# A Strassen MLP trunk: sums of weights and of squares moved to GpSimd, gating done straight from PSUM, the last products paired, and TensorE's order written out

## The chip, the core and the metric

The kernel runs on one core of one Trainium2 chip. The metric is device time in microseconds for one execution, the median of several runs. TensorE is PE in the rows (its weight loads PEld), VectorE is DVE, ScalarE is ACT, GpSimd is POOL, SyncE, which issues the DMAs, is SP.

## What is computed

One layer of a hybrid decoder trunk for 1024 prompt tokens and 32 sample tokens (8 sequences of 4), model width 1024, all in float32:

```python
h = rmsnorm(x, norm_mix_g) * (1 + sc1) + sh1
proj = h @ w_in                       # conv, gated recurrence and window attention heads
...                                   # the three head groups -> out_a, out_b, out_c
mix = jnp.concatenate([out_a, out_b, out_c.astype(x.dtype)], axis=-1) @ w_out
x = x + g1 * mix
h2 = rmsnorm(x, norm_mlp_g) * (1 + sc2) + sh2
x = x + g2 * (jnp.square(jax.nn.relu(h2 @ w_up)) @ w_down)
...
y_prompt = rmsnorm(xp, final_g)
```

The gates g1, g2 and the shifts are one vector for the whole prompt and one for each sample sequence. The change concerns what begins with `@ w_out`; the projection and the head groups ahead of it are not edited.

## The kernel before

Activations lie transposed in SBUF: a tile of [128, 8, 1056] holds 8 rows of 128 channels by 1056 tokens (1024 prompt, then 32 sample). The matrix products from `w_out` on are cut into nine **phases** of 1024 x 1024 weights: one for `w_out` ("out"), and four pairs for the MLP, up0, down0, up1, down1, up2, down2, up3, down3. Each phase is one level of Strassen's scheme: seven products of half size instead of eight, done in the order `SEQ = (2, 1, 6, 7, 4, 5, 3)`, each for four groups j of 128 output channels, so 28 **units** (p, j) in a phase. A float32 product is made of three reduced-precision matmuls (high x high, high x low, low x high, lines 1266 to 1268), for 4 blocks i of the inner dimension and 2 halves of 264 tokens: 24 matmuls in a unit, 672 in a phase.

Around each unit stands `prep`, which prepares what later units need:

- `w_unit(u)` splits the weights of unit u into a high and a low part (an ACT cast, line 1232, and a DVE subtraction, line 1233), three units ahead. Four such buffers rotate, so the weights of unit u+3 are split when product u-1 is done.
- `t_unit(p, i)` makes the activations of a product and splits them (ACT line 1252, DVE line 1253). Product 6 needs two further DVE subtractions, and a third that updates a block for product 4 (line 1255). The four up phases share their activations: up0 stores the split parts to HBM and up1 to up3 load them.
- `w_sums(ch)` makes Strassen's combinations of the weight blocks A, B, C, D in place, E = A - C, C = C + D, A = C - A, B = B - A (lines 1223 to 1226), for two halves ch of the columns, 1024 elements in each of 128 partitions. Products 6, 7 (E), 5 and 3 use the results.

`update` takes a product out of PSUM: an ACT copy for the first into a block in the phases that open a buffer, a DVE addition (line 1351) otherwise. PSUM is four buffers of two banks (pool `pp`).

In the out phase the result is added up in `hb`, and `gated` (line 1356) then adds g1 * hb to x, which is kept in `xr`. `norm2_square` squares it on ACT and adds up the squares on DVE (lines 1370 to 1374); `norm2(th)` turns the sums of one half th of the tokens into the reciprocal root (six small matmuls at line 1380, a DVE copy, two GpSimd instructions at lines 135 and 136, a DVE product `dg` with the identity, and a matmul with ones that spreads it over the partitions), and applies it to the eight rows (DVE line 1401, ACT line 1402) to give the input of up0 in `big_m`. `norm2(0)` is called after the first unit of product 5 of out, `norm2(1)` after the first unit of up0.

In down3 the products are gated into x, and the last rows are transposed back (line 1463), squared, normalised and stored, tile by tile of 128 tokens (`final_part`). The last product runs in two halves of 264 tokens.

The order of instructions on every engine comes from a scheduler that simulates engines and queues when the program is built. It may place an instruction ahead of others that come earlier in the code where it finds it ready. On the chip each engine works its list off in order.

Just ahead of the out phase stands the last part of the input projection, the gate of the recurrence (`evac_g`, lines 496 to 499), whose PSUM and scratch memory the phases then take over (`p1.close()`).

Of the kernel before, what the change touches and what calls it, by code (L numbers as in the profile page):

```python
# [19 lines left out]
P = 128  # L20
# [23 lines left out]
def kernel(  # L44
# [440 lines left out]

    def evac_g(h):
        def f_(c, ps):
# [701 lines left out]
    BLOCK = {"A": (0, 0), "B": (1, 0), "C": (0, 1), "D": (1, 1)}  # L1189

# [8 lines left out]

    class Phase:  # L1200
        def __init__(self, w, row0, col0, src=None, stored=None, keep=False, first=False):
            self.w, self.row0, self.col0 = w, row0, col0
            self.src, self.stored, self.keep, self.first = src, stored, keep, first
            self.raw, self.wu, self.tt = {}, {}, {}

        def w_tile(self, role):
            if role == ("B" if self.first else "E"):
                return rp.tile([P, D], F32, tag="wr", name="wr")
            return env["w2"].tile([P, D], F32, tag="wq", name="wq")

        def w_load(self, role):
            kh, nh = BLOCK[role]
            for ch in range(2):
                t = v3(self.w_tile(role), 256)
# [5 lines left out]
        def w_sums(self, ch):  # L1220
            a, b, c, d = (self.raw[r, ch] for r in "ABCD")
            e = self.raw["E", ch] = v3(self.w_tile("E"), 256)
            tt(out=e, in0=a, in1=c, op=ALU.subtract)
            tt(out=c, in0=c, in1=d, op=ALU.add)
            tt(out=a, in0=c, in1=a, op=ALU.subtract)  # L1225
            tt(out=b, in0=b, in1=a, op=ALU.subtract)

        def w_unit(self, u):
            p, j = SEQ[u // 4], u % 4
# [4 lines left out]
            self.wu[u] = t  # L1234
            if u in (5, 7):
                self.w_sums(u // 2 - 2)

        def t_unit(self, p, i):
# [15 lines left out]
            if p == 6:  # L1254
                tt(out=b21, in0=b21, in1=s, op=ALU.subtract)
# [16 lines left out]
    def bank2():  # L1272
        return env["pp"].tile([P, 1024], F32, tag="pp", name="pp")
# [4 lines left out]
    def flow(ph, nxt, update, order=None, after=lambda p, j: None, early=lambda u: None):  # L1278

        ps = {}  # L1280
        for i, p in enumerate(SEQ):
            for j in range(4):
                u = 4 * i + j
                if order is None or i < 5:
                    fresh = p in (2, 1, 5)
                    if fresh:
                        ps[j] = bank2()
                    ph.product(ps[j], p, j, fresh)
                    prep(ph, nxt, u)
                    update(p, j, ps[j])  # L1290
                    after(p, j)
        if order is not None:
            order(ph, nxt)

    def prep(ph, nxt, u):
        i, j = u // 4, u % 4
        q, v = (ph, i + 1) if i < 6 else (nxt, 0)
        if q is not None:
            q.t_unit(SEQ[v], j)
        q, v = (ph, u + 3) if u + 3 < 28 else (nxt, u + 3 - 28)  # L1300
        if q is not None:
            q.w_unit(v)
        if nxt is not None:
            for at, role in ((13, "B"), (18, "A"), (22, "C"), (25, "D")):
# [4 lines left out]
    ph_o = Phase(w_out, 0, 0, src=big_m, first=True)  # L1309
    for i, (w, fn) in enumerate(plan):  # L1310
# [15 lines left out]
    for u in range(3):  # L1326
        ph_o.w_unit(u)
# [258 lines left out]
```

## Time and profile before

| | us |
|---|---|
| median of 3 runs | 1295.61 (1294.93 to 1298.15) |
| the profiled execution, own time | 1299.38 |
| its span, first to last instruction | 1297.5 |
| matmul busy time | 1238.5 (95% of the span) |
| DVE, ACT, POOL busy | 907.6, 557.0, 69.1 |

The profiled execution lies 3.77 us above the median. Times within it are counted from its first instruction. The nine phases begin at 482.84 us. Matmuls overlap in the records, so that the spacing of their starts, not their recorded length, says how fast TensorE goes.

### The profile page before, as it was taken

To read this page: it belongs to the slowest core of one execution; us is meant where nothing else is said; L and a number is where in the kernel's file an instruction comes from. 1 tells how busy PE (TensorE), PEld (TensorE's weight loads), DVE (VectorE), ACT (ScalarE), POOL (GpSimd) and SP (SyncE) were. 2 spreads that over 40 slices of the span, in tenths; PEclk is the share of its full clock that TensorE was granted. 3 is DMA by queue.
4 is the path that set the end of the run, shared out by engine and by line. 5 is a ranking of instruction groups with operands and counts; after the bars stand their busy time and mean duration, and the time that the engine had idled before them with its cause. 6 is when DMAs were issued, how large, how long until landed. Compare 5 with 4: busy or idle time off the path is not lost.

```text
span 1297.5 us, 26603 instructions
## 1 busy us (share of the span) xinstructions
PE 1238.5 (95%) x10994; PEld 1170.4 (90%) x10994; DVE 907.6 (70%) x1651; ACT 557.0 (43%) x1127; POOL 69.1 (5%) x139
## 2 busy tenths in 40 slices
PE   8999999999999978985999999999999999999896
PEld 6889988888887978985999999999999999999896
DVE  4779995675746667697859554497643986528986
ACT  5622212433532343654665524553245632446332
POOL 3400000101200000000000000000000000000002
PEclk9999999999999999997999999999999999999899
DMA  8934333233132135222750275501666138561003
GB/s 272 366 106 125 99 102 96 76 107 96 56 99 85 36 137 176 86 99 115 298 200 18 66 248 205 196 17 50 203 230 216 34 99 282 207 227 50 1 1 135
DMA packets 116780, 172.44 MB, mean 133 GB/s; under 512 B 10877, under 2 KB 90835, under 8 KB 116636
## 3 DMA queue, kind: packets, MB, share of 16 engines
q1 hardware_dynamic: 116660, 170.74, 39.4%
q8 instruction: 87, 1.43, 0.5%
q14 instruction: 33, 0.27, 0.1%
HBM read 139.82 MB, written 32.13 MB: 133 GB/s over the span
## 4 chain that ended last, share of the span: by engine, by line
PE 73%; DVE 16%; DMA 5%; issue 3%; ACT 2%; SPq 1%; POOL 1%; DVEq 0%; ACTq 0%; POOLq 0%
PE pp L1268 13%; PE pp L1266 13%; PE pp L1267 13%; PE psg L157 7%; PE psg L158 7%; PE psg L159 7%; DVE tu L1253 3%; DMA wq<-in_w_down_dram 3%; DVE wu L1233 3%; PE pa_bank L259 2%; DVE xr L1351 1%; PE pso L849 1%; PE pso L622 1%; DVE wq L1225 1%; DVE t L1249 1%
## 5 line engine op out<-in xcount | busy, mean ns | idle before, releaser
L1266 PE MATMUL pp<-tu,wu 128*128 128x264 f32 x2016 | 580.6, 289 | 21.9 <-DVE H L497 7.3
L1267 PE MATMUL pp<-tu,wu 128*128 128x264 f32 x2016 | 580.6, 288 | 6.6 <-DVE tu L1253 6.6
L1268 PE MATMUL pp<-tu,wu 128*128 128x264 f32 x2016 | 578.2, 288 | 2.2 <-DVE wu L1233 2.1
L1266 PEld LDWEIGHTS pp<-tu,wu 128*128 128x128 f32 x2016 | 385.3, 191 | 24.9 <-issue 15.6
L1267 PEld LDWEIGHTS pp<-tu,wu 128*128 128x128 f32 x2016 | 385.5, 191 | 8.0 <-DVE tu L1253 7.9
L1268 PEld LDWEIGHTS pp<-tu,wu 128*128 128x128 f32 x2016 | 385.6, 192 | 4.1 <-DVE wu L1233 3.9
L1233 DVE TENSOR_TENSOR wu<-wq,wu 128x512 fp32r<-128x512 f32 x212 | 145.4, 687 | 107.6 <-ACT wu L1232 107.1
L1232 ACT CAST wu<-wq 128x512 fp32r<-128x512 f32 x212 | 130.8, 619 | 134.1 <-PE pp L1268 117.8
L157 PE MATMUL psg<-hh,wh 128*128 128x352 f32 x544 | 180.3, 333 | 0.7 <-ACT wh L148 0.7
L158 PE MATMUL psg<-hl,wh 128*128 128x352 f32 x544 | 176.7, 325 | 0.0
L159 PE MATMUL psg<-hh,wl 128*128 128x352 f32 x544 | 176.6, 325 | 0.0
L157 PEld LDWEIGHTS psg<-hh,wh 128*128 128x128 f32 x544 | 101.9, 188 | 12.2 <-issue 6.6
L158 PEld LDWEIGHTS psg<-hl,wh 128*128 128x128 f32 x544 | 102.4, 188 | 4.4 <-issue 4.0
L159 PEld LDWEIGHTS psg<-hh,wl 128*128 128x128 f32 x544 | 102.2, 188 | 3.4 <-issue 2.4
L1351 DVE TENSOR_TENSOR xr<-pp,xr 128x528 f32<-128x528 f32 x88 | 61.9, 704 | 26.9 <-PE pp L1268 26.9
L549 DVE SCALAR_TENSOR_TENSOR big_m<-big_m,vT 128x1024 f32<-128x1024 f32 x60 | 75.2, 1280 | 0.1
L1253 DVE TENSOR_TENSOR tu<-big_m,tu 128x528 fp32r<-128x528 f32 x96 | 64.4, 702 | 6.5 <-ACT tu L1252 6.5
L1252 ACT CAST tu<-big_m 128x528 fp32r<-128x528 f32 x96 | 55.6, 629 | 21.6 <-PE pp L1268 20.4
L135 POOL TENSOR_SCALAR s<-s 128x1 f32<-128x1 f32 (+4 forms) x39 | 9.7, 249 | 981.2 <-ACT yo L1468 684.1
L148 ACT CAST wh<-wr 128x1024 fp32r<-128x1024 f32 x24 | 25.1, 1046 | 67.2 <-PE psg L158 64.5
L1349 ACT COPY hb<-pp 128x528 f32<-128x528 f32 x40 | 24.0, 599 | 62.6 <-PE pp L1268 62.5
L1233 DVE TENSOR_TENSOR wu<-wr,wu 128x512 fp32r<-128x512 f32 x40 | 27.3, 688 | 32.0 <-ACT wu L1232 31.8
(337 smaller groups left out, 1470.8 us busy)
## 6 DMA issues: line engine op xcount, KB each, us to landing
tu<-th SPq DMA_DIRECT2D x84, 528.0 KB
ar<-in_w_ada_dram SPq DMA_DIRECT2D x32, 512.0 KB
wq<-in_w_up_dram SPq DMA_DIRECT2D x32, 512.0 KB
wq<-in_w_down_dram SPq DMA_DIRECT2D x32, 512.0 KB
th<-tu SPq DMA_DIRECT2D x28, 528.0 KB
wr<-in_w_in_dram SPq DMA_DIRECT2D x22, 512.0 KB
W<-in_w_ada_dram SPq DMA_DIRECT2D x32, 256.0 KB
xsp<-big_m SPq DMA_DIRECT2D x8, 528.0 KB
```

The source lines that it names most:

```text
L157: mm(pt, lhsT=wh[:, k, :], rhs=a, start=(first and i == 0), stop=False)
L158: mm(pt, lhsT=wh[:, k, :], rhs=b, start=False, stop=False)
L159: mm(pt, lhsT=wl[:, k, :], rhs=a, start=False, stop=(last and i == len(order) - 1))
L549: stt(out=pr, in0=ap[:, j : j + NP], scalar=w(j), in1=pr, op0=ALU.mult, op1=ALU.add)
L1232: scopy(t[:, 0], raw)
L1233: tt(out=t[:, 1], in0=raw, in1=t[:, 0].bitcast(F32), op=ALU.subtract)
L1252: scopy(t[:, 0], s)
L1253: tt(out=t[:, 1], in0=s, in1=t[:, 0].bitcast(F32), op=ALU.subtract)
L1266: mm(o, lhsT=w[:, 0, i], rhs=t[:, 0], start=fresh and i == 0, stop=False, skip_group_check=not fresh)
L1267: mm(o, lhsT=w[:, 0, i], rhs=t[:, 1], start=False, stop=False, skip_group_check=not fresh)
L1268: mm(o, lhsT=w[:, 1, i], rhs=t[:, 0], start=False, stop=i == 3, skip_group_check=not fresh)
L1351: tt(out=v, in0=pv(ps), in1=v, op=ALU.add)
```

## The change

- `w_sums` becomes `sums_ec` and `sums_ab`, on GpSimd (`ptt`) instead of DVE, each at a unit of its own: E and C at units 24 and 26 of the phase before (in out at 0 and 1, in up0 at 2 and 4), A and B at units 2 and 4. The update for product 4 in `t_unit` goes to GpSimd too. Weight blocks have fixed slots and are loaded up to four units earlier (units 9, 13, 17, 21).
- In out, block A is loaded before the last projection unit, and products 2's activations and the first two weights are prepared there. `issue_after` holds the work of the phases behind the last evacuations of the projection.
- PSUM becomes two pools of two buffers. TensorE's order is the order of the code from here on (`manual_schedule`).
- `gate` adds g1 times the product from PSUM to x, without `hb` in between (products 6, 7, 4, 5, 3 of out; 5 and 3 of down3). The sample tokens are collected apart in `ys` and finished by `samples`.
- The last two products of out are paired, 5 and 3 in the order (5,0) (5,1) (3,0) (3,1) (5,2) (5,3) (3,2) (3,3).
- The squares are added on GpSimd, and `norm2` is split into `norm2_sum` and `norm2_apply`, one unit apart: for the first half after units (5,1) and (3,0) of out, for the second after units 1 and 2 of up0. The spread factor is first copied to SBUF.
- In up0, product 6 runs with the inner block i as the outer loop (`product_rows`).
- In down3 the last product is cut into 416 and 112 tokens instead of 264 and 264.

```diff
+    PAIRED = PLAIN[:20] + [(5, 0), (5, 1), (3, 0), (3, 1), (5, 2), (5, 3), (3, 2), (3, 3)]
...
+    ptt = nc.gpsimd.tensor_tensor
...
-        def w_sums(self, ch):
-            a, b, c, d = (self.raw[r, ch] for r in "ABCD")
-            e = self.raw["E", ch] = v3(self.w_tile("E"), 256)
-            tt(out=e, in0=a, in1=c, op=ALU.subtract)
-            tt(out=c, in0=c, in1=d, op=ALU.add)
-            tt(out=a, in0=c, in1=a, op=ALU.subtract)
-            tt(out=b, in0=b, in1=a, op=ALU.subtract)
+        def sums_ec(self, ch):
+            e = self.raw["E", ch] = v3(self.slots["E"][ch], 256)
+            a, c, d = (self.raw[r, ch] for r in "ACD")
+            ptt(out=e, in0=a, in1=c, op=ALU.subtract)
+            ptt(out=c, in0=c, in1=d, op=ALU.add)
+
+        def sums_ab(self, ch):
+            a, b, c = (self.raw[r, ch] for r in "ABC")
+            ptt(out=a, in0=c, in1=a, op=ALU.subtract)
+            ptt(out=b, in0=b, in1=a, op=ALU.subtract)
...
             if p == 6:
-                tt(out=b21, in0=b21, in1=s, op=ALU.subtract)
+                ptt(out=b21, in0=b21, in1=s, op=ALU.subtract)
...
+        def product_rows(self, ps, p):
+            for i in range(4):
+                for j in range(4):
+                    for c in range(2):
+                        self.part(ps[j][:, c * 512 : c * 512 + HC], p, j, i, c * HC, (c + 1) * HC, False)
...
+        return env["ppA" if n % 4 < 2 else "ppB"].tile([P, 1024], F32, tag="pp", name="pp")
...
+            ph_o.slots["A"] = [W(D) for _ in range(2)]
+            ph_o.w_load("A")
             for k in range(4):
                 ph_o.t_unit(2, k)
+            for u in range(2):
+                ph_o.w_unit(u)
...
+    ctx.enter_context(tc.manual_schedule(engines={mybir.EngineType.PE}))
+    behind = ExitStack()
+    for ins in last_ev:
+        behind.enter_context(tc.issue_after(ins.ins))
...
+    def gate(n, th, src, g0):
+        v = two(hv(xr, n, th))
+        stt(out=v, in0=src, scalar=mod[:, g0 + n, 0:1], in1=v, op0=ALU.mult, op1=ALU.add)
...
+        act(dst, v, AF.Square)
+        if not first:
+            ptt(out=acc[th][:, :w], in0=acc[th][:, :w], in1=dst, op=ALU.add)
...
+        rb = tmp()
+        scopy(two(rb), pv(ps))
...
+            tt(out=big_m[:, k, a], in0=xr[:, k, a], in1=rb[:, :w], op=ALU.mult)
+            act(big_m[:, k, a], big_m[:, k, a], AF.Identity, scale=s2[:, k, 0:1], bias=mod[:, 24 + k, 0:1])
...
+        cut = 5 * P - HT
```

**The start of the phases, on DVE.** The rows stand where the last gate of the projection is taken out of PSUM (`H<-H,psg` and `big_m<-big_m,H`, 320 prompt and 32 sample tokens for each of two heads). `tu` and `wu` are split activations and weights of the out phase, `big_m<-big_m` are Strassen's combinations of activations. Before:

```order
L1233 TENSOR_TENSOR wu<-wr,wu 128x512
L497 SCALAR_TENSOR_TENSOR H<-H,psg 128x320
L1247 TENSOR_TENSOR big_m<-big_m 128x528
L1233 TENSOR_TENSOR wu<-wr,wu 128x512
L1247 TENSOR_TENSOR big_m<-big_m 128x528
L1233 TENSOR_TENSOR wu<-wr,wu 128x512 x2
L499 TENSOR_TENSOR big_m<-big_m,H 128x320
L497 SCALAR_TENSOR_TENSOR H<-H,psg 128x32
L497 SCALAR_TENSOR_TENSOR H<-H,psg 128x320
L1251 TENSOR_TENSOR big_m<-big_m 128x528 x2
```

Now, at the same place:

```order
L1249 TENSOR_TENSOR wu<-wr,wu 128x512
L499 SCALAR_TENSOR_TENSOR H<-H,psg 128x320
L1249 TENSOR_TENSOR wu<-wr,wu 128x512
L501 TENSOR_TENSOR big_m<-big_m,H 128x320
L499 SCALAR_TENSOR_TENSOR H<-H,psg 128x32
L501 TENSOR_TENSOR big_m<-big_m,H 128x32
L499 SCALAR_TENSOR_TENSOR H<-H,psg 128x320
L501 TENSOR_TENSOR big_m<-big_m,H 128x320
L499 SCALAR_TENSOR_TENSOR H<-H,psg 128x32
L501 TENSOR_TENSOR big_m<-big_m,H 128x32
L1388 SCALAR_TENSOR_TENSOR s_113<-mod,vT 128x72
```

The combinations of activations no longer stand between the evacuations of the two heads; they come behind them.

**The weight sums of out, on POOL.** The wq tiles are the slots of the weight blocks (5886 and 5887 are C, 5888 and 5889 are D, 5890 and 5891 become E), W holds A. POOL had nothing in this place before. Now:

```order
L1269 TENSOR_TENSOR big_m<-big_m,t 128x528
L1236 TENSOR_TENSOR wq_5890<-W,wq_5886 128x1024
L1236 TENSOR_TENSOR wq_5891<-W,wq_5887 128x1024
L1269 TENSOR_TENSOR big_m<-big_m,t 128x528
L1237 TENSOR_TENSOR wq_5886<-wq_5886,wq_5888 128x1024
L1269 TENSOR_TENSOR big_m<-big_m,t 128x528
L1237 TENSOR_TENSOR wq_5887<-wq_5887,wq_5889 128x1024
L1269 TENSOR_TENSOR big_m<-big_m,t 128x528
L1241 TENSOR_TENSOR W<-wq_5886,W 128x1024
L1387 COPY xs<-xr 128x256
L1241 TENSOR_TENSOR W<-wq_5887,W 128x1024
```

The new A, which product 6 needs first (line 1241), is the ninth of these.

**The first half of the norm, on DVE.** `s<-pp` is the copy of the summed squares, `dg` the diagonal, and then come the eight rows that are normalised (line 1401 before, 1480 now). Before:

```order
L1382 COPY s<-pp 88x6
L1360 TENSOR_TENSOR xr<-s,xr 128x32
L1351 TENSOR_TENSOR hb<-pp,hb 128x528 x2
L1385 TENSOR_TENSOR dg<-ident,s 88x528
L1233 TENSOR_TENSOR wu<-wr,wu 128x512
L1356 SCALAR_TENSOR_TENSOR xr<-hb,mod,xr 128x496
L1223 TENSOR_TENSOR wr<-wq 128x1024
L1351 TENSOR_TENSOR hb<-pp,hb 128x528 x2
L1233 TENSOR_TENSOR wu<-wr,wu 128x512
L1224 TENSOR_TENSOR wq<-wq 128x1024
L1356 SCALAR_TENSOR_TENSOR xr<-hb,mod,xr 128x496
L1401 SCALAR_TENSOR_TENSOR t<-xr,s_113,pp 128x528 x4
```

Now:

```order
L1461 COPY s<-pp 88x6
L1405 SCALAR_TENSOR_TENSOR xr<-pp,mod,xr 128x528
L1439 TENSOR_TENSOR ys<-pp,ys 128x32
L1249 TENSOR_TENSOR wu<-wr,wu 128x512
L1464 TENSOR_TENSOR dg<-ident,s 88x528
L1480 TENSOR_TENSOR big_m<-xr,t 128x528 x8
L1405 SCALAR_TENSOR_TENSOR xr<-pp,mod,xr 128x528
L1439 TENSOR_TENSOR ys<-pp,ys 128x32
L1267 TENSOR_TENSOR tu<-big_m,tu 128x528
L1249 TENSOR_TENSOR wu<-wr,wu 128x512
L1267 TENSOR_TENSOR tu<-big_m,tu 128x528
L1405 SCALAR_TENSOR_TENSOR xr<-pp,mod,xr 128x528
```

The weight sums are gone from between, all eight rows are normalised in one run, and the gates (line 1405) of the units behind (3,0) stand behind that run. Each row now reads two SBUF operands (`xr` and `t`) where it read one from PSUM.

## Rows read from the trace of the kernel before

**Rows 1.** The page, busy time of each engine and its share of the span.

```profile
PE 1238.5 (95%) x10994; PEld 1170.4 (90%) x10994; DVE 907.6 (70%) x1651; ACT 557.0 (43%) x1127; POOL 69.1 (5%) x139
```

**Rows 2.** By stretch: length, busy PE, PEld, DVE, ACT, POOL, clock, DMA share, GB/s.

```profile
482.80:508.30 25.50, 25.46 (x191) 25.49 (x192) 17.80 (x23) 7.62 (x13) 0.00 (x0) 0.91 0.61 212
508.30:529.00 20.70, 16.08 (x96) 14.45 (x95) 17.86 (x29) 11.27 (x21) 0.00 (x0) 0.84 0.28 91
529.00:578.20 49.20, 49.20 (x405) 48.86 (x404) 39.10 (x61) 28.74 (x51) 1.52 (x2) 1.00 0.32 104
578.20:689.80 111.60, 92.58 (x691) 90.02 (x690) 85.03 (x141) 65.79 (x115) 1.52 (x2) 0.91 0.52 191
689.80:772.00 82.20, 82.02 (x674) 81.81 (x673) 58.30 (x87) 38.83 (x69) 0.00 (x0) 1.00 0.30 98
772.00:854.00 82.00, 82.00 (x674) 82.00 (x673) 41.37 (x58) 43.97 (x76) 0.00 (x0) 1.00 0.55 191
854.00:939.80 85.80, 84.27 (x675) 83.76 (x674) 67.15 (x101) 30.57 (x52) 0.00 (x0) 0.98 0.29 94
...
1188.60:1254.00 65.40, 62.05 (x485) 61.62 (x484) 62.89 (x111) 25.52 (x45) 0.00 (x0) 0.95 0.01 1
1254.00:1288.80 34.80, 32.15 (x264) 30.88 (x262) 24.98 (x63) 9.57 (x18) 4.80 (x12) 1.00 0.23 91
1288.80:1297.50 8.70, 0.00 (x0) 0.00 (x0) 3.65 (x3) 2.85 (x6) 2.17 (x6) 0.74 0.36 137
```

**Rows 3.** Waits of PE from 460 us on: total us, times, longest.

```profile
PE pp L1380 <- DVE t L1374: 8.8, 1, 8.8
PE pp L1266 <- DVE H L497: 7.3, 1, 7.3
PE pp L1267 <- DVE tu L1253: 6.6, 5, 2.9
PE pp L1266 <- DVE xr L1351: 5.9, 3, 2.9
```

**Rows 4.** Timeline of PE, 475.0 to 487.8 us: start, length, instruction, idle before.

```profile
475.04 0.32 PE L158 MATMUL psg<-hl,wh 128*128 128x352 f32 x1
475.20 0.32 PE L159 MATMUL psg<-hh,wl 128*128 128x352 f32 x1
...
482.84 0.56 PE L1266 MATMUL pp<-tu,wu 128*128 128x264 f32 x1 [7.31 <-DVE H L497]
...
487.15 0.42 PE L1267 MATMUL pp<-tu,wu 128*128 128x264 f32 x1
487.37 0.33 PE L1268 MATMUL pp<-tu,wu 128*128 128x264 f32 x1
487.54 0.29 PE L1266 MATMUL pp<-tu,wu 128*128 128x264 f32 x1
487.66 0.28 PE L1267 MATMUL pp<-tu,wu 128*128 128x264 f32 x1
```

**Rows 5.** Groups by line and shape, DVE from 475 us on: busy us, mean ns.

```profile
L1233 DVE TENSOR_TENSOR wu<-wq,wu 128x512 fp32r<-128x512 f32 x212 | 145.4, 687 | 107.6 <-ACT wu L1232 107.1
L1224 DVE TENSOR_TENSOR wq<-wq 128x1024 f32<-128x1024 f32 x18 | 22.0, 1224 | 17.8 <-DMA wq<-in_w_down_dram 10.6 <-DMA wq<-in_w_up_dram 6.1 <-DMA wq<-in_w_out_dram 1.0
```

**Rows 6.** Groups by line and shape, POOL, whole run.

```profile
L347 POOL TENSOR_TENSOR hl<-H,hh 128x320 fp32r<-128x320 f32 x5 | 4.9, 995 | 3.3 <-ACT hh L339 3.3
L136 POOL TENSOR_TENSOR s<-s,mhalf 88x6 f32<-88x6 f32 x2 | 2.6, 1320 | 0.2
...
L317 POOL TENSOR_TENSOR hl<-H,hh 128x64 fp32r<-128x64 f32 x4 | 1.9, 465 | 4.9 <-ACT hh L316 4.9
```

**Rows 7.** Timelines of POOL and DVE, 57.4 to 62 us, in the projection.

```profile
57.55 0.87 POOL L347 TENSOR_TENSOR hl<-H,hh 128x320 fp32r<-128x320 f32 x1 [0.66 <-ACT hh L339]
...
57.63 1.17 DVE L336 SCALAR_TENSOR_TENSOR H<-big_m,s,W 128x352 f32<-128x352 f32 x1
...
61.50 0.54 DVE L336 SCALAR_TENSOR_TENSOR H<-big_m,s,W 128x320 f32<-128x320 f32 x1
```

More of the change, by code (lines that the diff above doesn't have):

```diff
@@ L1272, in bank2, with flow @@
     def bank2():
-        return env["pp"].tile([P, 1024], F32, tag="pp", name="pp")
+        n = env["n"] = env.get("n", -1) + 1
+        return env["ppA" if n % 4 < 2 else "ppB"].tile([P, 1024], F32, tag="pp", name="pp")
     def pv(ps):
         return v3(ps, 512)[:, :, :HC]
-    def flow(ph, nxt, update, order=None, after=lambda p, j: None, early=lambda u: None):
+    def flow(ph, nxt, update, tail=None, after=lambda p, j: None, rows=()):
         ps = {}
[L1281 to L1293, printed above, removed]
+        if nxt is not None:
+            nxt.slots_from(ph)
+        for u, (p, j) in enumerate(ph.units):
+            if tail is not None and u == 20:
+                tail(ph, nxt)
+                return
+            fresh = p in (2, 1, 5)
+            if fresh:
+                ps[j] = bank2()
+            if p not in rows:
+                ph.product(ps[j], p, j, fresh)
+            prep(ph, nxt, u)
+            if p in rows and j == 0:
+                ph.product_rows(ps, p)
+            update(p, j, ps[j])
+            after(p, j)
@@ L1302, in prep @@
             q.w_unit(v)
+        for ch in range(2):
+            if ph.sums and u == ph.sums[ch]:
+                ph.sums_ec(ch)
+            if u == 2 + 2 * ch:
+                ph.sums_ab(ch)
+            if nxt is not None and not nxt.sums and u == 24 + 2 * ch:
+                nxt.sums_ec(ch)
         if nxt is not None:
-            for at, role in ((13, "B"), (18, "A"), (22, "C"), (25, "D")):
+            for at, role in ((9, "B"), (13, "A"), (17, "C"), (23 if ph.units is PAIRED else 21, "D")):
                 if u == at:
@@ L1518 @@
+        pt = {t: bank2() for t in (5, 6)}
+        pb = bank2()
+        pt.update({t: bank2() for t in (7, 8, 4)})
+        for j in range(4):
+            ps = pb[:, j * cut : (j + 1) * cut]
+            for i in range(4):
+                ph.part(ps, 3, j, i, 0, cut, True)
+            v = xr[:, j, HT : 5 * P]
+            stt(out=v, in0=ps, scalar=mod[:, G2 + j, 0:1], in1=v, op0=ALU.mult, op1=ALU.add)
+            final(5 + j, pt[5 + j], K_LATE)
+        final(4, pt[4], K_LATE)
     for g in range(G8):
```

307 lines of the change are left out of this document (161 added, 146 removed).

## Prediction

> **What bounds the kernel now.** The first look is at the engines' shares: TensorE's matmuls cover 95% of the span, DVE's work 70%, POOL's 5% [rows 1]. So time is won where TensorE stands still or runs slowly, and POOL is nearly free. The second look is at the stretches, one per phase or part of one [rows 2]. Where nothing disturbs it, a phase of 672 matmuls takes 82.0 us (772 to 854, clock 1.00); that is 2.93 us for a unit of 24. Against it: out has its first eight units in 25.5 us (23.4 undisturbed), units 8 to 11 in 20.7 (11.7), the last sixteen in 49.2 (46.9); up0 takes 111.6, 29.6 more than undisturbed; down0 82.2; down1 85.8 (down2, like it, is not shown again); the first twenty units of down3 65.4 instead of 58.6; then 34.8 to the last transposed rows and 8.7 to the end. The third look is at TensorE's waits by what ended them [rows 3]: 8.8 us once for the sum of squares, 7.3 once for the last evacuation of the projection, 6.6 for split activations, 5.9 for DVE's additions out of PSUM. All of them are waits for DVE. The fourth is the timeline at the first of them [rows 4]: the last projection matmul starts at 475.20, the first of out at 482.84 after 7.31 us idle; then matmuls of 264 columns start 0.22 us apart up to 487.37 and 0.12 apart from 487.54 on. That is the clock at its lower level (1.2 instead of 2.4 GHz) after an idle stretch: the first 4.5 us, 20 matmuls, cost 2.0 us more. The 0.91, 0.84 and 0.95 in [rows 2] are the same cost behind other stalls. A stall of some us costs about 1.7 us on top.
>
> **The price of a sum on GpSimd.** On DVE a 1024-column sum takes 1.22 us [rows 5]. GpSimd does 320 columns in 0.995 us and 64 in 0.465 [rows 6]: 2.07 ns a column, so 2.4 us for 1024 and 1.4 for 528 (estimates). But there is more. At 57.55 GpSimd ran one with 320 columns for 0.87 us; DVE's instruction at 57.63, also with two SBUF inputs, took 1.17 us for 352 columns, where one with 320 columns took 0.54 [rows 7]. It ended 0.38 us after GpSimd's, less than its own length, so it was held back until about 0.2 us before GpSimd's end: GpSimd holds DVE off for 0.7 of its 0.87 us, 2.2 of 2.4 us for 1024 columns, 1.2 of 1.4 for 528. The Trainium skill says so too, on the page SBUF — State Buffer, section Who interferes with whom: a DVE instruction with two SBUF inputs and a GpSimd instruction that reads SBUF exclude each other, and the later one blocks; the row agrees (1.17 against 0.54). By that page alone every GpSimd sum is paid by DVE at nearly its full length, which speaks against this change; what that would cost is the slower rival below.
>
> **A phase's account.** DVE gives up eight sums and, where activations are made, four updates: 8 x 1.22 + 4 x 0.70 (a 528-column operation costs little more than the 0.69 of 512 [rows 5]) = 12.6 us. GpSimd's holds are 8 x 2.2 + 4 x 1.2 = 22.4 us. What of them hits DVE depends on how often DVE then reads PSUM or is idle: in down1 it is busy 67.2 of 85.8 us [rows 2], and about a quarter of its 101 instructions there are additions out of PSUM. I take half, 11 us. So the sums by themselves relieve DVE by 1 to 2 us a phase, no more; bounds are 12.6 us relieved (no hold hits) and 9.8 lost (each does).
>
> **(a) Start to unit 12 of out.** By the new order the evacuations stand ahead of the combinations, and the first activations and weights are ready before the last projection matmul ends. The 7.3 us wait and its 2.0 us of slow clock go. But DVE's work for units up to 8 is the same, and starts no earlier. Behind the last evacuations (some 1.8 us, an estimate for eight instructions, half of them on 32 tokens) DVE has 39 instructions in its new order up to the weights of unit 8: 39 x 0.69 = 27 us, so unit 8 starts 29 us after 475.5 at best. GpSimd has four sums and four updates to do before the new A; half of their holds, (4 x 2.2 + 4 x 1.2) / 2 = 6.8 us, makes it 36. Before, it was at 508.3, 32.8 us after. I take 32.5: the stall at the start is late again at unit 8. What remains is the 9 us that units 8 to 11 lost before (20.7 against 11.7): the new A blocks come one behind the other on POOL, so the four weights are then ready together. Against it 1.7 us for the clock after the new stall. That gives -8 us, bounds -13 and -4.
>
> **(b) The last sixteen units of out.** They lost 2.3 us, two small norm matmul groups included. Now the spread matmul stands one unit, 2.9 us, after the sums. Its chain is a copy, two GpSimd instructions (1.32 us for the second [rows 6]) and `dg`; by the order `dg` stands behind the gate of (3,0), which waits for that unit's end; then come the gate, a short sample addition, a weight split and `dg`, at 0.69 for each long one and a little for the short one 2.3 us (estimate). TensorE waits for that. Behind it eight rows are normalised, 8 x 0.70 = 5.6 us, ahead of the next gates; unit (3,2) needs one of them, and with two GpSimd sums of up0 falling there it is up to 4.4 us late. With half of that, the clock and the matmuls it is +4 us, bounds +2 and +8. The pairing hides the rest: a unit of product 3 adds to the PSUM buffer that the gate of product 5 must first read, and one other unit, 2.9 us, lies between, against under 1.4 for the two DVE instructions.
>
> **(c) up0.** Its loss of 29.6 us is mostly the two norms. Now the first is done in out, and the second starts after unit 1. But activations of unit 4 stand, by the order, behind all eight rows of the second half: the spread matmuls are done at 10.7 us of the phase (three units and 2 us of norm matmuls); then one ACT copy and, on DVE, eight rows, two short sample steps and two further instructions, twelve steps at up to 0.7, so 19 us, where unit 4 wants them at 15. And the weights of unit 11 stand behind some 25 more DVE instructions, 36.6 us against 31.9 wanted. With 2 us of norm matmuls and 3 of slow clock it loses 14 us without holds, and 23 with those of four sums and four updates on top. I take 17: -13 us, bounds -25 (the holds fall into waits and TensorE waits for one chain alone, 5 us) and -7.
>
> **(d) down0 to down3, up to unit 20.** They lost 0.2 + 3.8 + 3.2 + 6.8 = 14 us. By the account above DVE's load is nearly the same. -1, bounds -12 and +15. The up phases lost nothing, DVE is busy half the time in them, and a weight split has three units of lead: 0.
>
> **(e) The end.** 34.8 us for eight units and 72 transposes. Spacing is 0.12 for 264 columns and 0.16 for 352 [rows 4], so 0.186 for 416 (estimate) and 0.06 to 0.12 for 112: 48 x 0.186 + 48 x 0.06 to 0.12 = 11.8 to 14.7, where two halves took 11.7. So the cut itself saves no matmul time; it lets four tiles' transposes run between the short parts. The stores' chain behind the last transposes (8.7 us) stays. DVE, busy 25 of 34.8, has eight gates instead of sixteen half gates. -2, bounds -4 and +1.
>
> The other edits (slots, early loads, split PSUM pools) cost nothing as long as loads land ahead of GpSimd's sums; DMA shares of 0.29 to 0.61 leave room. If a load is late, TensorE waits behind GpSimd's fixed list; no row prices that.
>
> **Sum.** -8 + 4 - 13 - 1 - 2 = -20 on the profiled execution's own 1299.4 us: 1279.4. That execution lies 3.8 us over the median, so 1275.6 is predicted.
>
> **The rivals.**
>
> *Holds hardly matter.* GpSimd's sums fall where DVE waits for TensorE anyway. For it speaks that DVE idles in the second half of each phase; against it that it was busy in nearly all of units 24 to 10 of the down phases. Then -13 + 2 - 20 - 10 - 4 = -45: 1250.6.
>
> *The start stays.* TensorE's first unit still waits, for PSUM buffers or activations, and the new order does not do what it says there: (a) is 0, 1283.6. The order of rows speaks against it.
>
> *Gain and loss cancel.* (a) -4, (b) +8, (c) -9, (d) +4, (e) -1: -2, 1293.6.
>
> *Slower: DVE is blocked by GpSimd.* Each hold delays DVE at its full length in the down phases, where DVE is behind at units 8 to 11 already. Then a down phase loses 9.8 us of DVE time, and less the 3 us of lead that a unit has, 7 in each of the last three: (d) +20, with (a) -4, (b) +8, (c) -7, (e) -2: +15, 1310.6. It decides from the point where 20 of the 22 us of holds hit DVE. The quarter of DVE's instructions that read PSUM speaks against it. The Trainium skill's rule on the page SBUF — State Buffer (Who interferes with whom), taken without anything that lies beside the holds, comes out here; by that rule, the trace agrees on the block itself, not on how often it falls.
>
> **Chances.** My forecast 0.57, hardly any holds 0.20, the start stays 0.06, cancelled 0.08, slower 0.09. A change of under 0.3% (3.9 us) can't be told from none here. Faster: 0.83; the same: 0.08; slower: 0.09. The range from 1249 to 1300 leaves out the slower rival and the upper and lower ends of the others.
>
> **What would show it.** Right: the first out matmul within 1 us of the last projection matmul; a stall of several us at unit 8 of out that ends with a GpSimd sum or a weight split; DVE instructions with two SBUF inputs lengthened to 2 us and more beside GpSimd's sums, those out of PSUM not; up0 at 95 to 105 us with stalls at units 4 and 8 to 11; down1 to down3 within 4 us of before. Wrong: up0 under 90 us, or no stall at unit 8 (DVE less behind than its order suggests), or down phases above 90 us.

## The result, and the profile after

The changed kernel takes 1327.76 us (1327.39 to 1328.29, 4 runs), the kernel before 1296.06 (1294.93 to 1298.15, 4 runs): a ratio of 1.0243, 95% interval 1.0225 to 1.0261. It is slower by 31.7 us, where 1275.6 was forecast. The profiled execution has a span of 1325.8 us, 28.3 more than before's; the other 3.4 us are that before's profiled execution lay over its median and this one does not. Ratios compare fast executions alone: one slow execution of the kernel with pieces (1323.95 us) and one of the kernel with late E (5076.3 us) count in the medians below and not in the ratios, and without them these medians would be 1305.68 and 1277.04.

The page's first rows, next to [rows 1], show POOL at 26% and DVE's time hardly less, with 136 instructions fewer:

```profile
PE 1245.8 (94%) x10994; PEld 1178.5 (89%) x10994; DVE 903.1 (68%) x1515; ACT 554.9 (42%) x1126; POOL 344.4 (26%) x251
```

The stretches that answer to [rows 2], same columns: units 0 to 7 of out with the wait for unit 8, units 8 to 11, the last sixteen; up0; down0; down1; the first twenty units of down3; the end.

```profile
476.20:523.40 47.20, 23.95 (x195) 23.53 (x193) 45.18 (x43) 16.37 (x31) 39.77 (x16) 0.80 0.50 179
523.40:540.40 17.00, 14.92 (x97) 14.62 (x98) 10.20 (x15) 5.69 (x13) 1.62 (x1) 0.75 0.13 39
540.40:595.20 54.80, 52.25 (x403) 51.40 (x402) 41.01 (x59) 30.50 (x55) 24.06 (x14) 0.94 0.29 99
595.20:705.10 109.90, 92.71 (x691) 90.39 (x690) 81.96 (x104) 62.57 (x109) 41.19 (x20) 0.91 0.51 186
705.10:790.90 85.80, 83.96 (x675) 83.73 (x674) 52.81 (x73) 37.76 (x68) 33.71 (x12) 0.98 0.29 94
872.80:961.80 89.00, 85.06 (x673) 84.66 (x673) 67.06 (x89) 30.03 (x52) 28.12 (x12) 0.96 0.28 91
...
1214.70:1280.00 65.30, 61.31 (x482) 60.84 (x481) 65.23 (x102) 25.05 (x44) 17.90 (x8) 0.95 0.00 1
1280.00:1325.80 45.80, 34.85 (x266) 33.54 (x264) 28.89 (x51) 13.01 (x23) 7.95 (x18) 0.98 0.24 95
```

TensorE's longest waits from 460 us on, next to [rows 3]:

```profile
PE pp L1275 <- ACT wu L1248: 22.1, 1, 22.1
PE pp L1277 <- DVE wu L1249: 12.9, 9, 2.2
PE pp L1275 <- DVE xr L1401: 7.3, 3, 2.5
```

The wait of 7.3 us at the start is gone. In its place stands one of 22.1 us, for the cast of unit 8's weights on ACT. What happens ahead of it is seen in the timelines of POOL, DVE and ACT (start, length, instruction, idle before):

```profile
483.55 8.96 POOL L1269 TENSOR_TENSOR big_m<-big_m,t 128x528 f32<-128x528 f32 x1 [21.34 <-ACT wu L1248]
492.46 5.21 POOL L1236 TENSOR_TENSOR wq<-W,wq 128x1024 f32<-128x1024 f32 x2
...
508.36 2.81 POOL L1241 TENSOR_TENSOR W<-wq,W 128x1024 f32<-128x1024 f32 x1
...
511.96 2.35 POOL L1241 TENSOR_TENSOR W<-wq,W 128x1024 f32<-128x1024 f32 x1
514.27 1.76 POOL L1423 TENSOR_TENSOR hb<-hb 128x528 f32<-128x528 f32 x1
515.99 5.57 POOL L1242 TENSOR_TENSOR wr<-wr,W 128x1024 f32<-128x1024 f32 x2
```

```profile
489.38 0.70 DVE L1263 TENSOR_TENSOR t<-big_m 128x528 f32<-128x528 f32 x1
490.00 1.32 DVE L1265 TENSOR_TENSOR big_m<-big_m 128x528 f32<-128x528 f32 x2
492.54 2.89 DVE L1263 TENSOR_TENSOR t<-big_m 128x528 f32<-128x528 f32 x1 [1.22 <-POOL big_m L1269]
495.35 2.87 DVE L1249 TENSOR_TENSOR wu<-W,wu 128x512 fp32r<-128x512 f32 x1
498.15 1.82 DVE L1267 TENSOR_TENSOR tu<-t,tu 128x528 fp32r<-128x528 f32 x1
499.88 0.69 DVE L1401 TENSOR_TENSOR hb<-pp,hb 128x528 f32<-128x528 f32 x1
...
516.52 2.85 DVE L1267 TENSOR_TENSOR tu<-big_m,tu 128x528 fp32r<-128x528 f32 x1
519.29 2.84 DVE L1405 SCALAR_TENSOR_TENSOR xr<-hb,mod,xr 128x528 f32<-128x528 f32 x1
```

```profile
516.63 0.64 ACT L1421 ACTIVATE hb<-xr 128x528 f32<-128x528 f32 x1 [3.16 <-DVE xr L1405]
522.16 0.64 ACT L1421 ACTIVATE hb<-xr 128x528 f32<-128x528 f32 x1 [4.89 <-DVE xr L1405]
522.71 2.16 ACT L1248 CAST wu<-W 128x512 fp32r<-128x512 f32 x4
```

Three things are to be seen. First, from 492 us on a DVE instruction with two SBUF operands ends some 0.56 us behind the GpSimd instruction that it meets: 2.84 to 2.89 us beside a sum of 1024 columns, 1.82 beside one of 528, where alone it takes 0.70. The addition out of PSUM (line 1401) stays at 0.69. DVE gets one such instruction done for each of GpSimd's. Second, it holds the other way too: GpSimd's first update takes 8.96 us, because DVE works without a break until 491.3. Third, at unit 8 TensorE does not wait for GpSimd's result. The half of the new A that unit 8 uses is ready at 511.2 (508.36 + 2.81), the other at 514.3; the casts come at 522.71, since on ACT they stand behind the square of the last gated row (522.16), which waits for DVE's gate (line 1405), which GpSimd holds.

In down0 it is otherwise: there an update on GpSimd is shut out by DVE for some 7 us, the sums behind it come late, and ACT's cast of unit 10's weights waits for the new A (POOL and ACT):

```profile
715.84 8.48 POOL L1269 TENSOR_TENSOR hb<-hb,t 128x528 f32<-128x528 f32 x1 [4.94 <-DVE t L1263]
...
730.74 2.84 POOL L1241 TENSOR_TENSOR wr<-wq,wr 128x1024 f32<-128x1024 f32 x1
...
733.61 0.62 ACT L1248 CAST wu<-wr 128x512 fp32r<-128x512 f32 x1 [5.75 <-POOL wr L1241]
```

Unit 10 of down0 then takes 6.6 us instead of 2.9. And in up0 the matmuls of the norm wait 2.1 us for a sum of squares on GpSimd. So late results cost something too.

### The profile page after: what moved, and what is told of

Same layout as the page of the kernel before. It is cut to its first block, busy times and chain, and to the rows that moved or that the text cites. A ratio compares the mean times of both kernels' runs of the same rounds, so it can differ in the third digit from the quotient of the medians.

```text
span 1325.8 us, 26655 instructions
## 1 busy us (share of the span) xinstructions
PE 1245.8 (94%) x10994; PEld 1178.5 (89%) x10994; DVE 903.1 (68%) x1515; ACT 554.9 (42%) x1126; POOL 344.4 (26%) x251
## 4 chain that ended last, share of the span: by engine, by line
PE 72%; DVE 17%; issue 4%; POOL 2%; DMA 2%; ACT 2%; SPq 0%; DVEq 0%; ACTq 0%; POOLq 0%
PE pp L1277 13%; PE pp L1276 13%; PE pp L1275 13%; PE psg L157 7%; PE psg L158 7%; PE psg L159 7%; DVE tu L1267 4%; DVE wu L1249 4%; PE pa_bank L259 1%; PE pso L852 1%; PE pso L625 1%; DVE xr L1401 1%; DVE big_m L1265 1%; DMA W<-in_x_prompt_dram 1%; DVE xr L1530 1%
## 5 line engine op out<-in xcount | busy, mean ns | idle before, releaser
L1275 PE MATMUL pp<-tu,wu 128*128 128x264 f32 (+1 forms) x2016 | 585.0, 290 | 39.2 <-ACT wu L1248 22.1
L1277 PE MATMUL pp<-tu,wu 128*128 128x264 f32 (+1 forms) x2016 | 584.3, 290 | 12.9 <-DVE wu L1249 12.9
L1276 PE MATMUL pp<-tu,wu 128*128 128x264 f32 (+1 forms) x2016 | 584.9, 290 | 4.1 <-DVE tu L1267 4.1
L1277 PEld LDWEIGHTS pp<-tu,wu 128*128 128x128 f32 x2016 | 389.3, 193 | 15.2 <-DVE wu L1249 15.1
L1249 DVE TENSOR_TENSOR wu<-wq,wu 128x512 fp32r<-128x512 f32 x184 | 152.4, 829 | 109.8 <-ACT wu L1248 109.3
L1248 ACT CAST wu<-wq 128x512 fp32r<-128x512 f32 x184 | 113.6, 619 | 147.7 <-PE pp L1277 127.7
L1267 DVE TENSOR_TENSOR tu<-big_m,tu 128x528 fp32r<-128x528 f32 x96 | 81.9, 876 | 21.3 <-ACT tu L1266 21.3
L1401 DVE TENSOR_TENSOR xr<-pp,xr 128x528 f32<-128x528 f32 x88 | 61.7, 701 | 49.2 <-PE pp L1277 49.2
L1249 DVE TENSOR_TENSOR wu<-wr,wu 128x512 fp32r<-128x512 f32 x60 | 51.1, 852 | 26.4 <-ACT wu L1248 26.1
L1266 ACT CAST tu<-big_m 128x528 fp32r<-128x528 f32 x96 | 56.9, 630 | 23.4 <-PE pp L1277 22.2
L1248 ACT CAST wu<-wr 128x512 fp32r<-128x512 f32 x60 | 37.0, 620 | 57.9 <-PE pp L1277 37.2
```

Source lines behind the costliest of these rows:

```text
L1248: scopy(t[:, 0], raw)
L1249: tt(out=t[:, 1], in0=raw, in1=t[:, 0].bitcast(F32), op=ALU.subtract)
L1266: scopy(t[:, 0], s)
L1267: tt(out=t[:, 1], in0=s, in1=t[:, 0].bitcast(F32), op=ALU.subtract)
L1275: mm(out, lhsT=w[:, 0, i], rhs=t[:, 0], start=fresh and i == 0, stop=False, skip_group_check=not fresh)
L1276: mm(out, lhsT=w[:, 0, i], rhs=t[:, 1], start=False, stop=False, skip_group_check=not fresh)
```

## Experiments

Four theories stood against each other: exclusion (1), the fixed order and other parts of the change (2), late GpSimd results alone (3), and for the end a wait of its own. Times are medians of 4 to 10 runs; ratios are to the kernel before on the same chip. The first four kernels ran on one chip, the next four on another, the last two on a third, where the kernel before took 1297.8, 1297.6 and 1300.0 us, so a difference in us across chips is good to some 2 us. The table of stretches under the experiments belongs to all of them.

**All sums back on DVE.**

```diff
-    ptt = nc.gpsimd.tensor_tensor
+    ptt = nc.vector.tensor_tensor
```

> The changed kernel with all the moved sums back on DVE, everything else of the change kept. Theory 1 (exclusion: while GpSimd works on a sum with two SBUF operands, DVE's instructions with two SBUF operands stand still for its whole length, in the changed trace 2.85 us instead of 0.69): unit 8 of out starts some 38 us after the last projection matmul instead of 47, the down phases come back by the 3.5 us that each of the last three lost (and 3.6 in down0), no DVE instruction of 512 columns takes over 1 us; in all 1327.8 - 9 - 14 - 5 = about 1300, 1285 to 1308. Theory 2 (TensorE's fixed order, the pairing and the split norm cost the time, the sums do not): 1320 to 1335, down phases unchanged at 86 to 89 us. Theory 3 (only the lateness of the GpSimd results, which run one behind the other at 2.8 us each, and no block of DVE): unit 8 of out comes back too, but the down phases, where no matmul waits for a GpSimd result, stay at 86 to 89: about 1315.

1284.99 us, ratio 0.9910 (0.9875 to 0.9945): 43 us faster than the changed kernel and faster than the kernel before. Theory 2 falls: nothing but the sums' engine differs in the code, and TensorE's list is the same (the lists of DVE and ACT are put together anew by the scheduler). Down1 takes 82.9 us instead of 89.1; with GpSimd's results merely late (theory 3) it should have stayed.

**Only the weight sums back on DVE.**

```diff
-            ptt(out=e, in0=a, in1=c, op=ALU.subtract)
+            tt(out=e, in0=a, in1=c, op=ALU.subtract)
...
```

> The changed kernel with only the weight sums (72 of 1024 columns) back on DVE; the block updates for product 4 and the additions of squares stay on GpSimd. Theory 1 (exclusion, full length): the weight sums are 72 x 2.8 = 202 us of GpSimd's work, the rest 39 x 1.8 = 70 us, so most of what the all-DVE kernel gains is here too: 1303 to 1312. Theory 2 (order of TensorE): 1320 to 1335. Theory 3 (late results only): the new A of out is no longer late, so about 1315.

1294.37 us, ratio 0.9971 (0.9951 to 0.9990): 9.4 us over the all-DVE kernel, for the 39 short sums left on GpSimd. That lies under the range of theory 1 (1303 to 1312) as well as those of the others.

**Only the weight sums on GpSimd.**

```diff
-                ptt(out=b21, in0=b21, in1=s, op=ALU.subtract)
+                tt(out=b21, in0=b21, in1=s, op=ALU.subtract)
...
-            ptt(out=acc[th][:, :w], in0=acc[th][:, :w], in1=dst, op=ALU.add)
+            tt(out=acc[th][:, :w], in0=acc[th][:, :w], in1=dst, op=ALU.add)
...
```

> The changed kernel with the block updates for product 4, the additions of squares and the small sample product back on DVE; only the weight sums stay on GpSimd. Theory 1: 202 of the 270 us of holds stay, 1318 to 1325; up0 and the end of out get back some us, since the sums of squares of the norm stand no longer in GpSimd's list between weight sums. Theory 2: 1320 to 1335. Theory 3: the new A of out comes four updates (7 us) earlier, so 1320.

1300.97 us, ratio 1.0026 (1.0004 to 1.0048): 16 over the all-DVE kernel, far less than expected: all three theories had it at 1318 or more. 9.4 and 16 make 25, both together cost 43. The costs don't add up; in down1 too they are 0.8 and 3.0 alone and 6.2 together. Why is not shown by a run of its own.

**The kernel before, weight sums on GpSimd.**

```diff
-            tt(out=e, in0=a, in1=c, op=ALU.subtract)
+            nc.gpsimd.tensor_tensor(out=e, in0=a, in1=c, op=ALU.subtract)
...
```

> The kernel before with one edit, its weight sums on GpSimd instead of DVE, where they stood (behind the weight splits of units 5 and 7). Theory 1: DVE gives up 72 x 1.22 = 88 us and is held for up to 72 x 2.8 = 202; where it is behind, in units 0 to 11 of out, up0 and the down phases, time is lost: 1310 to 1330. Theory 2 (the sums on GpSimd do no harm, TensorE's order does): 1280 to 1296. Theory 3 (late results only): out and each phase wait at unit 8 for A, which comes 3 x 2.8 us after its inputs: 1300 to 1315, with stalls at unit 8 alone and no lengthened DVE instruction.

1304.0 us, ratio 1.0063 (1.0037 to 1.0089): the sums do harm without any other part of the change. The time lies under the range of theory 1 and in that of theory 3, but the trace decides against 3: DVE's weight splits take 896 ns in the mean instead of 687 [rows 5].

```profile
L1233 DVE TENSOR_TENSOR wu<-wq,wu 128x512 fp32r<-128x512 f32 x212 | 189.8, 896 | 120.2 <-ACT wu L1232 119.5
```

**Shadows that nobody waits for.**

```diff
...
+    def shadow(v):
+        parts = [v[:, :, k * 104 : k * 104 + 104] for k in range(2)] if len(v.shape) == 3 else [v[:, :416]]
+        for u in parts:
+            s = v3(env["scr"], 104) if len(v.shape) == 3 else env["scr"]
+            nc.gpsimd.tensor_tensor(out=s, in0=u, in1=u, op=ALU.add)
+    def ptt(out, in0, in1, op, sh=None):
+        tt(out=out, in0=in0, in1=in1, op=op)
+        shadow(out if sh is None else sh)
...
```

> All sums on DVE, as in the run that measured 1285.0, and GpSimd does a shadow of each: it adds the result to itself (two SBUF operands, two pieces of 416 columns for a weight sum, one of 416 for the others, 183 in all) into a scratch tile that nobody reads. No matmul and no DVE instruction takes anything from GpSimd, so whatever is lost is lost by GpSimd's running at the same time. Theory 1 (exclusion, one DVE instruction for each GpSimd instruction): DVE's instructions with two SBUF operands beside a shadow take about 1.5 us (the shadow's own length) instead of 0.69, those out of PSUM stay at 0.69; the loss of the three later down phases comes back and unit 8 of out is late again: 1315 to 1345. Theory 3 (GpSimd's results only come late): 1285 to 1289, no DVE instruction longer. In between, 1295 to 1310: the block is real, but part of the 42 us between the changed kernel and the all-DVE one came from the late results.

1325.59 us, ratio 1.0218 (1.0184 to 1.0253): 40.6 us lost to work that gives nothing to anybody: no wait in this trace ends with a shadow, and DVE's instructions, 1626 in both kernels, are busy for 975.6 us instead of 906.1. So theory 1 holds: the block alone can cost as much as the change did. How the changed kernel's own 43 us divide between the block and the late results of down0 and the norm, this does not show. Three groups of DVE by line and shape, from 470 us on (busy us, mean ns, idle before):

```profile
L1258 DVE TENSOR_TENSOR wu<-wq,wu 128x512 fp32r<-128x512 f32 x184 | 141.9, 773 | 106.9 <-ACT wu L1257 106.3
L1411 DVE TENSOR_TENSOR hb<-pp,hb 128x528 f32<-128x528 f32 x28 | 19.6, 699 | 5.3 <-PE pp L1286 5.2
L1415 DVE SCALAR_TENSOR_TENSOR xr<-hb,mod,xr 128x528 f32<-128x528 f32 x4 | 4.2, 1067 | 0.0
```

The same groups of the all-DVE kernel:

```profile
L1249 DVE TENSOR_TENSOR wu<-wq,wu 128x512 fp32r<-128x512 f32 x184 | 126.4, 688 | 110.8 <-ACT wu L1248 110.2
L1401 DVE TENSOR_TENSOR hb<-pp,hb 128x528 f32<-128x528 f32 x28 | 19.6, 702 | 7.6 <-PE pp L1277 7.4
L1405 DVE SCALAR_TENSOR_TENSOR xr<-hb,mod,xr 128x528 f32<-128x528 f32 x4 | 3.0, 762 | 0.0
```

The two-operand groups grow (688 to 773, 762 to 1067 ns), the one out of PSUM does not (702 and 699). The Trainium skill, page SBUF — State Buffer, section Who interferes with whom, says just this of a DVE instruction with two SBUF inputs beside a GpSimd instruction that reads SBUF; the runs agree.

**Shadows as copies.**

```diff
-            nc.gpsimd.tensor_tensor(out=s, in0=u, in1=u, op=ALU.add)
+            nc.gpsimd.tensor_copy(s, u)
```

> As the kernel with shadows, but each shadow is a GpSimd copy (one SBUF operand) of the same columns. Theory 1a (any GpSimd work on SBUF excludes DVE's two-operand instructions): a loss in proportion to the copies' length, 1.2 to 1.5 us for 416 columns by the 0.87 us of the 256-column copy in the changed kernel's trace: 1305 to 1335. Theory 1b (only GpSimd instructions with two operands exclude): 1285 to 1290 with DVE's instructions at 0.69. Theory 3: 1285 to 1289.

1302.25 us (1295.50 to 1307.17), ratio 1.0028 (1.0000 to 1.0056): theory 1a, in a smaller size, under its range. The profiled execution is the fastest of the ten, nearly 7 us under the median. A copy with one SBUF operand excludes as well, but it is shorter (0.83 us in the mean), so a DVE instruction beside one takes 1.03 us:

```profile
500.89 1.03 DVE L1276 TENSOR_TENSOR tu<-big_m,tu 128x528 fp32r<-128x528 f32 x1
501.84 1.03 DVE L1415 SCALAR_TENSOR_TENSOR xr<-hb,mod,xr 128x528 f32<-128x528 f32 x1
502.79 0.70 DVE L1276 TENSOR_TENSOR tu<-big_m,tu 128x528 fp32r<-128x528 f32 x1
```

**GpSimd's sums in pieces.**

```diff
...
+            for k in range(4):
+                nc.gpsimd.tensor_tensor(out=out[:, k], in0=in0[:, k], in1=in1[:, k], op=op)
...
```

> The changed kernel with each GpSimd sum cut into pieces: 1024 columns as 4 of 256, 528 as 2 of 264; the sums stay on GpSimd. Theory 1 (one DVE instruction passes for each GpSimd instruction): a DVE instruction beside the pieces takes 0.9 to 1.4 us instead of 2.85, so DVE runs at half its speed instead of a quarter, and GpSimd's sums take 4 to 5 us instead of 2.8 where DVE is busy. As the two take turns, the sum of both works stays, and only what waits for what changes: weight splits and activations come earlier, the new A blocks later; 1305 to 1335, most likely a little faster than the changed kernel's 1327.8. Theory 3 (late results, no block): four times the fixed cost makes GpSimd's list longer, so slower: 1330 to 1350, and DVE's instructions stay as they are.

1305.98 us, ratio 1.0062 (1.0042 to 1.0082): 22 us faster than with whole sums, at the lower end of theory 1's range, though POOL's busy time grew from 344.4 to 432.5 us. DVE's fell from 903.1 to 862.4. DVE passes one instruction per piece, at 1.23 us instead of 2.85:

```profile
492.41 1.23 DVE L1274 TENSOR_TENSOR t<-big_m 128x528 f32<-128x528 f32 x1 [1.36 <-POOL big_m L1220]
493.57 1.23 DVE L1260 TENSOR_TENSOR wu<-W,wu 128x512 fp32r<-128x512 f32 x1
...
517.98 2.40 DVE L1260 TENSOR_TENSOR wu<-W,wu 128x512 fp32r<-128x512 f32 x2 [8.46 <-ACT wu L1259]
```

And here theory 3's wait does appear: DVE is idle for 8.46 us behind ACT's cast, whose own idle time ends with GpSimd's new A.

```profile
517.33 1.14 ACT L1259 CAST wu<-W 128x512 fp32r<-128x512 f32 x2 [9.44 <-POOL W L1216]
```

**The tail's order, all sums on DVE.**

```diff
-        for j in range(4):
+        for j in (0, 2, 1, 3):
             ps = pa[j // 2][:, j % 2 * 512 : j % 2 * 512 + HT - cut]
```

> All sums on DVE (1285.0), and in the last product the four parts of 416 columns go in the order 0, 2, 1, 3 instead of 0, 1, 2, 3. In the trace of the all-DVE kernel the second and the fourth wait 2.40 and 0.90 us for DVE's short sample product (line 1581) out of the same PSUM buffer, though out of its other bank. Theory: a matmul into one half of such a two-bank buffer waits until the other half is read; with the new order another part of 2 us lies between, the two waits go, and with them the clock's fall behind the first: -3 to -5 us, 1280 to 1282. Rival (the wait is for DVE's place in its list, not for the buffer): the waits move to the second part in the new order, no gain, 1284 to 1287.

1279.22 us, ratio 0.9855 (0.9824 to 0.9887). By the traces, from unit 20 of down3 to the end, 49.0 us became 45.6: -3.4, and from the first matmul of the last product, where the edit begins, 31.5 became 26.7: -4.9. TensorE's waits in that stretch, in the all-DVE kernel:

```profile
PE pp L1275 <- DVE s L1581: 3.3, 2, 2.4
PE pp L1544 <- DVE xr L1530: 2.0, 1, 2.0
```

and with the new order only the second of them is left:

```profile
PE pp L1544 <- DVE xr L1530: 2.0, 1, 2.0
```

So a matmul into one half of a two-bank buffer did wait until the other half had been read. In all kernels with the old order of the parts the stretch behind that first matmul is 29.9 to 31.5 us, in the three with the new one 26.4 to 26.7. The rest of the difference to the all-DVE kernel lies ahead of the edit: in this profiled execution the projection ended 4.2 us earlier.

**E behind the new A in out.**

```diff
...
+        def sum_e(self, ch):
+            ptt(out=self.raw["E", ch], in0=self.raw["D", ch], in1=self.raw["A", ch], op=ALU.subtract)
...
+            if ph.sums == (0, 1) and u == 8 + ch:
+                ph.sum_e(ch)
```

> The kernel with all sums on DVE and the tail order 0, 2, 1, 3 (1279.2), and in out alone the two sums E of 1024 columns, needed from unit 12 on, come behind the new A blocks, as E = D - A (new A) at units 8 and 9 instead of A - C at units 0 and 1. Theory (unit 8 of out starts when DVE has worked off its list, whatever stands in it): two sums less ahead of the weight splits of units 8 and 9, 2 x 1.22 us; units 7 and 8, which take 12.8 and 9.2 us in the kernel without this edit, lose 2.4 us together, and nothing is lost later, where DVE has time: 1276.8, out at 101.5 us instead of 103.9. Rival (unit 8 waits for something else, the loads of the weight blocks or the activations): out stays at 103.5 to 104, 1279.

1277.1 us, ratio 0.9828 (0.9785 to 0.9871). Units 7 and 8 of out take 6.1 and 13.5 us instead of 12.8 and 9.2: -2.4 together, as forecast; out as a whole went from 103.9 to 100.1, 1.4 more than that. With the sums on DVE, unit 8 waits for DVE's list. More moved in it than the two sums: the first half of A is done 26.0 us behind the last projection matmul instead of 32.7, unit 8 starts 6.7 us earlier, and its own 4.3 us more give most of that back. The forecast had the total and not its parts.

**And the norm one unit later in up0.**

```diff
-        if (p, j) == (2, 1):
+        if (p, j) == (2, 2):
             norm2_sum(1)
-        if (p, j) == (2, 2):
+        if (p, j) == (2, 3):
             norm2_apply(1)
```

> As the kernel with the late E, and in up0 the sum and the spread of the second half of the norm stand one unit later (behind units 2 and 3 instead of 1 and 2). In the trace without this edit, TensorE waits 2.95 us at that sum for DVE's additions of squares, and later for activations and weights of units 4 and 8. Theory: from unit 1 to unit 8 of up0 DVE works without a break, so the wait of units 1 and 2 only moves to units 4 and 8: up0 stays within 1.5 us of 100.3. Rival (the norm's chain is what up0 waits for): the 2.95 us are won, and unit 1 with it: up0 at 96 to 98. A loss is possible too, if product 6's activations wait for the rows one unit longer: 102 to 104.

1274.38 us, ratio 0.9824 (0.9786 to 0.9863), not to be told from the run before it. Up0 takes 100.8 us against 99.9: the wait only moved, from units 1, 2, 4 and 8 (8.1, 5.2, 8.1, 7.1 us) to units 2, 3, 7 and 8 (6.5, 6.2, 7.2, 10.4). DVE sets the pace there.

The stretches, in us, between first matmuls of units in the timelines of TensorE (projection: its last matmul; down: the four down phases, down3 up to unit 20; end: from there to the span's end):

| kernel | projection to unit 12 of out | to up0 | up0 | down1 | down, all | end |
|---|---|---|---|---|---|---|
| before | 54.3 | 48.9 | 111.5 | 85.8 | 318.2 | 43.7 |
| changed | 64.3 | 54.8 | 109.9 | 89.1 | 329.0 | 45.8 |
| all on DVE | 51.7 | 52.0 | 100.0 | 82.9 | 308.5 | 49.0 |
| weights on DVE | 55.7 | 54.3 | 102.9 | 83.7 | 311.0 | 46.6 |
| weights alone on GpSimd | 57.5 | 50.4 | 104.3 | 85.9 | 319.6 | 45.0 |
| before, weights on GpSimd | 56.9 | 51.9 | 112.3 | 85.9 | 316.0 | 42.8 |
| shadows, two operands | 55.9 | 53.6 | 110.8 | 88.7 | 332.0 | 49.2 |
| shadows, copies | 53.1 | 53.6 | 104.7 | 85.0 | 316.0 | 47.5 |
| pieces | 57.5 | 56.0 | 106.1 | 84.7 | 317.2 | 46.4 |
| all on DVE, tail order | 52.0 | 52.0 | 100.3 | 82.8 | 308.4 | 45.6 |
| and late E | 49.0 | 51.2 | 99.9 | 82.8 | 308.4 | 44.0 |
| and norm later | 49.2 | 51.3 | 100.8 | 82.9 | 308.5 | 41.5 |

The up phases behind up0 are 81.8 to 82.1 us in all of them.

## Why the prediction was wrong, step by step

The forecast sum was -20 us; the span grew by 28.3. By the table: +0.9 for a later end of the projection, +10.0 for (a), +5.9 for (b), -1.6 for (c), +10.7 for (d) and 0.3 in the up phases, +2.1 for (e). The same terms with all sums on DVE are +0.9 and -2.6, +3.2, -11.5, -9.8 and 0.3, +5.2, in all -14.3. So without GpSimd's sums the change is a gain, near the 20 us forecast, though this nearness is luck: (a) and (e) gave 5 and 7 us less than forecast, (d) 9 more. The step that failed is the price of the holds, "I take half".

**The account of a phase.** As an average it was right. The 111 sums take 114.4 us on DVE in the all-DVE kernel (their groups summed); without them its 906.1 us would leave 791.7, and the changed kernel has 903.1. GpSimd's holds thus cost DVE 111.4 us, 41% of the 274.3 us that POOL's time grew by, and the relief that came out is 3.0 us over the nine phases (906.1 to 903.1), 0.3 a phase, a little less than the "1 to 2 us" of the account. But TensorE does not wait for the average. It waits where DVE has a row of instructions without a break, and there almost all have two SBUF operands; the quarter that reads PSUM does not help, since what stands behind each is held again.

**(a)** was right in form: the first matmul of out is at 476.26, 0.2 us behind the projection's last, and the stall is at unit 8. It failed by size, in the sentence "four sums and four updates to do before the new A; half of their holds ... = 6.8 us". Ahead of unit 8 POOL did eight sums, four updates, three additions of squares and a copy, and DVE's 43 instructions took 45.18 us, 1.05 each; the all-DVE kernel has 0.66 each over the same length:

```profile
476.30:524.70 48.40, 35.30 (x264) 34.78 (x264) 45.38 (x69) 20.75 (x39) 0.42 (x1) 0.82 0.50 178
```

43 x 0.39 = 17 us of holds (an estimate, since the all-DVE kernel has other instructions in that stretch) instead of 6.8. With 17 the forecast's own sum, 29 us without holds, gives 46, and unit 8 starts 47.3 us behind the last projection matmul. Its 6.8 had given 36, for which the text took 32.5, about what the kernel before had, without a reason. And the last link was not the new A but the gates held by the sums behind it.

**(b)** +4 forecast, +5.9 measured, inside its bounds. The waits for the spread matmul (2.3 us) and behind it are where they were expected.

**(c)** -13 forecast, -1.6 measured, outside its bounds. The working had both ends, a loss of 14 us without holds and 23 with all of them; measured against 82 they are 18.0 (all on DVE) and 27.9. Both are 4 to 5 us too low, and "I take 17" took the middle where the upper end held. The stalls are at units 4 and 8, as said (8.7 and 15.2 us).

**(d)** -1 forecast, +10.7 measured, near the upper bound of +15. In down1 to down3 it is for the reason of the slower rival: units 5 and 6 of down1 take 5.5 and 7.1 us. In down0, 3.5 us slower than before, it is unit 10, behind the late A. What the forecast missed on the other side is that the same code with the sums on DVE gains 9.8 us there.

**(e)** The cut was forecast at -2 and made the end longer, by 2.1 us here and 5.2 with all sums on DVE. Part of that, 3.3 to 3.4 us by the waits of the two traces, is the wait of a 416-column part for the other half of its PSUM buffer, which the step did not look for. From the first matmul of the last product on, before takes 27.3 us, the changed kernel 30.1, and the three kernels with the new order 26.4 to 26.7: without that wait the cut gains a little under 1 us. The whole end still varies between these three (45.6, 44.0 and 41.5 us, against before's 43.7) by their units 20 to 23, which none of the edits touches.

**The slower rival** had the mechanism, with a chance of 0.09 and a price of 1310.6. It asked for 20 of 22 us of holds in the down phases; there (d) lost 10.7 us of its 20, but by the table the sums on GpSimd also cost 12.6 us in (a) and 9.9 in (c) (changed against all on DVE), where the rival still had gains. What spoke against it, the instructions out of PSUM, was no protection.

## What to carry to other kernels

An idle GpSimd is no free engine for sums of two SBUF operands while DVE works on such operands too: moving a 1.22 us sum off DVE cost DVE up to 2.2 us of standing still. Price such a move in the stretches where the bound engine waits for DVE, at the full length there, not at the kernel's average. Where it must be, short pieces do less harm than whole sums (22 us here); and keep the other parts of such a change: with the sums left on DVE, and two small edits behind it (the tail's order and the late E), it is 1.7% faster than the kernel before.

## What the runs showed of the hardware

- Once a GpSimd sum is in, the two engines take turns, one instruction each. A GpSimd sum of 1024 columns took 2.40 us where DVE left it alone (774.88) and 2.81 where it alternated; 528 columns 1.31 and 1.76; 256 columns 0.71 and 1.19. Each turn of DVE costs GpSimd some 0.45 us, and DVE waits for GpSimd's whole instruction.
- DVE working on two SBUF operands without a break starves GpSimd: 8.96 us for an update of 1.31, and 8.37 for a sum of 2.40. The sum ended at 629.56, and 2.40 us before that, at 627.2, DVE had come to an addition out of PSUM.

```profile
774.88 2.40 POOL L1236 TENSOR_TENSOR wq<-wq,wq 128x1024 f32<-128x1024 f32 x1 [38.84 <-DMA wq<-in_w_up_dram]
621.19 8.37 POOL L1241 TENSOR_TENSOR wq<-wq,wq 128x1024 f32<-128x1024 f32 x1 [7.95 <-DVE wu L1249]
...
627.22 0.70 DVE L1401 TENSOR_TENSOR hb<-pp,hb 128x528 f32<-128x528 f32 x1
```
